# A chunked scan with scalar decays: the order of TensorE's work fixed by hand, one run of scan products per chunk

## The chip, the core and the metric

The kernel runs on one core of a Trainium2 chip as one program. The metric is the device time of one execution in microseconds. Before the change it is 3205.98 us, the median of three runs (3205.3 to 3206.26). The core's engines are named as the profile names them: PE (TensorE, with PEld for its weight loads), DVE (VectorE), ACT (ScalarE), POOL (GpSimd) and SP, whose queue issues most DMAs.

## The reference, cut to what matters

The program is three transformer-like blocks in sequence over 1024 positions and 1024 channels. The change touches the third block's second branch (`ssd_branch`): a causal depthwise convolution of width 4 with SiLU, a scan of 16 heads in 4 groups whose decays are scalars per head and position, and a gated group norm.

```python
xBC = silu(causal_depthwise_conv_3(xBC, conv_w, conv_b))   # xs (16 heads x 64), B and C (4 groups x 128)
dt = softplus(dt_raw + dt_bias);  A = -exp(A_log)
scores = einsum('bclhn,bcshn->bhcls', Ch, Bh) * exp(segsum(a))      # inside one chunk
y_diag = einsum('bhcls,bcshp->bclhp', scores, xd)
states = einsum('bclhn,bhcl,bclhp->bchpn', Bh, decay_states, xd)    # what a chunk adds to the state
y_off  = einsum('bclhn,bchpn,bhcl->bclhp', Ch, prev_states, exp(a_cs))
y = y_diag + y_off + Dh * xs
g = y * silu(z);  out = g * rsqrt(mean_group(g * g) + EPS) * norm_w
```

Beside it stands the S5 branch, of which only the last steps lie in the same stretch of time: a GELU per 128 channels (`gelu`) and a gated projection by `w_glu` (`glu`).

## The kernel before, in words

A weight of 1024 x 128 comes by DMA (`wraw`), is split by ACT (L147, `whi`) and POOL (L148, `wlo`) into two parts, and a dense half is 24 matmuls of 128 x 512 on PE (L157): 8 blocks of the contraction times three products. A group of four heads needs 12 dense halves: `conv_in` four times two (x, x, B, C) and the gate twice two (`rest`). Each half of `conv_in` leaves PSUM by a DVE product (L1710), then ACT, three DVE taps (L1715), ACT's tanh and a DVE product (L1718). A half of the gate is copied by ACT (L1743), turned by four PE transposes (L1745), scaled by ACT and passed through tanh. `to_time` turns x and B of a group in six PSUM banks of four transposes (L1728); each bank is copied out by DVE or ACT in turn (L1734, L1732), and there are two such banks (`tp`).

`scan` goes over 8 chunks of 128 positions. On PE a chunk has: the decay matrix (L1780 and two products L1786, whose operands ACT makes in L1785), B times C (L1790), the chunk's products for four heads (L1797, eight instructions), the state's output (L1802, two instructions, not in chunk 0) and the new state (L1810, two instructions, not in chunk 7). ACT's exponential and DVE's product (L1791) stand between L1786 and L1797; DVE's sum (L1814) stands between L1810 and the next chunk's L1802. `leave` turns the normed result (L1839) and writes it out.

The order of each engine's work is chosen by a planner, which runs through the program with durations of its own and takes, of what is ready by them, the instruction of the highest priority: what stands earlier in the program, and what is marked `high_priority` as if it stood 3000 places earlier. `scan(g)` is marked so; `project(g + 1)` (eight halves of `conv_in`, then `rest`) stands behind it and fills PE between the scan's products one matmul at a time. Dense halves also take one entry of a list (`K.tick`), by which the eight `gelu` steps are spread. A helper, `K.queue`, ties each PE instruction handed to it to the one before, while `K.queued` is set; in this branch it is not set. The engine's queue then keeps the planned order at run time.

In PSUM there are three `mm` banks for dense halves, two `aux`, two `tp` and one `stat`. `xt` and `bt` have one buffer, `M`, `sg`, `xd`, `st` and the gates `szt` two.

Of the kernel before, what the change touches and what calls it, by code (L numbers as in the profile page):

```python
# [1620 lines left out]
class SSD:  # L1621


    def __init__(self, K, norm, store, pd, pc):
        self.K, self.norm, self.store, self.pd, self.pc = K, norm, store, pd, pc
        self.mixd, self.groups = {}, {}
# [70 lines left out]
    def conv_in(self, g, i):  # L1697
# [6 lines left out]
        def ev(_, hf, ps):  # L1704
# [5 lines left out]
            nc.vector.tensor_mul(cp[:, 4:4 + HALF], ps, self.norm.row[hf])  # L1710
# [9 lines left out]
        K.dense([K.I["w_in_3"][col]], self.norm.y, ev)  # L1720

    def to_time(self, src, dst, at):
        K, nc = self.K, self.K.nc
        for b in range(2):
            pt = K.tp_bank()
            for i in range(4):
                c = 4 * b + i
                nc.tensor.transpose(pt[:, i * 128:(i + 1) * 128], src[:, c * 128:(c + 1) * 128], K.ident)  # L1728
# [7 lines left out]
    def rest(self, g, pool):  # L1736

        K, nc, y = self.K, self.K.nc, self.norm.y
        sz = pool.tile([128, 8, 256], F32, tag="szt", name=K.n("szt"), bufs=2)

        def ev(i, hf, ps):
            z = pool.tile([128, HALF], F32, tag="zf", name=K.n("zf"), bufs=1)
            nc.scalar.copy(z, ps)  # L1743
            for k in range(4):
                nc.tensor.transpose(ps[:, k * 128:(k + 1) * 128], z[:, k * 128:(k + 1) * 128], K.ident)  # L1745
            o = sz[:, 4 * hf:4 * hf + 4, i * 128:(i + 1) * 128]
            for k in range(4):
                nc.scalar.activation(o[:, k, :], ps[:, k * 128:(k + 1) * 128], AF.Copy, scale=self.zc[:, 4 * hf + k:4 * hf + k + 1])
            t2 = self.pc.tile([128, HALF], F32, tag="th", name=K.n("th"), bufs=2).rearrange("p (a b) -> p a b", b=128)
            K.act(t2, o, AF.Tanh)  # L1750
            nc.vector.scalar_tensor_tensor(o, t2, 1.0, o, op0=ALU.add, op1=ALU.mult)
            K.tick()

        K.dense([K.I["w_z_3"][2 * g + i] for i in range(2)], y, ev)
# [6 lines left out]
        self.groups[g] = t, xt, bt, sz  # L1761

    def project(self, g, pool):
        for i in range(4):
            self.conv_in(g, i)
        self.rest(g, pool)

    def scan(self, g, pool):
        K, nc = self.K, self.K.nc
        t, xt, bt, sz = self.groups[g]  # L1770
        CT, BT = t[3], t[2]
        hs = slice(4 * g, 4 * g + 4)
        h64 = lambda x: x.unsqueeze(2).to_broadcast((128, 4, 64))
        v64 = lambda x: x.rearrange("p (a b) -> p a b", b=64)
        st = None
        ss = pool.tile([128, 8], F32, tag="ss", name=K.n("ss"), bufs=2)
        for c in range(8):
            cs = slice(c * 128, (c + 1) * 128)
            ps = K.aux_bank()
            nc.tensor.matmul(ps.rearrange("p (a b) -> p a b", b=128), K.identb,  # L1780
                             self.future.unsqueeze(1).to_broadcast((128, 4, 128)), start=True, stop=False)
            for n, a in enumerate(self.ap):
                sg = pool.tile([128, 4, 128], F32R, tag="sg", name=K.n("sg"), bufs=2)
                for i in range(4):
                    nc.scalar.activation(sg[:, i, :], self.tri, AF.Copy, scale=a[:, c, 4 * g + i:4 * g + i + 1].bitcast(F32))  # L1785
                nc.tensor.matmul(ps, self.after1, sg.rearrange("p a b -> p (a b)"), start=False, stop=n == 1)  # L1786
            M = pool.tile([128, 4, 128], F32, tag="M", name=K.n("M"), bufs=2)
            K.act(M, ps.rearrange("p (a b) -> p a b", b=128), AF.Exp)
            pc = K.pp.tile([128, HALF], F32, tag="stat", name=K.n("cm"), bufs=1)
            nc.tensor.matmul(pc[:, 0:128], BT[:, cs], CT[:, cs], start=True, stop=True)  # L1790
            nc.vector.tensor_tensor(M, M, pc[:, 0:128].unsqueeze(1).to_broadcast((128, 4, 128)), op=ALU.mult)  # L1791
            x = xt[:, c, :]
            xd = pool.tile([128, 256], F32, tag="xd", name=K.n("xd"), bufs=2)
            nc.vector.tensor_tensor(v64(xd), v64(x), h64(self.dt[:, c, hs]), op=ALU.mult)
            yp = K.tp_bank()
            for i in range(4):
                nc.tensor.matmul(yp[:, i * 64:(i + 1) * 64], M[:, i, :], xd[:, i * 64:(i + 1) * 64], start=True, stop=True)  # L1797
            yo = pool.tile([128, 256], F32, tag="yo", name=K.n("yo"), bufs=2)
            nc.gpsimd.tensor_tensor(v64(yo), v64(x), h64(self.Dh[:, hs]), op=ALU.mult)
            nc.vector.tensor_add(yo, yp[:, 0:256], yo)  # L1800
            if c:
                nc.tensor.matmul(yp[:, 256:512], CT[:, cs], st, start=True, stop=True)  # L1802
                w = pool.tile([128, 256], F32, tag="yw", name=K.n("yw"), bufs=2)
                nc.vector.tensor_tensor(v64(w), v64(yp[:, 256:512]), h64(self.ecs[:, c, hs]), op=ALU.mult)
                nc.vector.tensor_add(yo, yo, w)
            if c < 7:
                xw = pool.tile([128, 256], F32, tag="xw", name=K.n("xw"), bufs=2)
                nc.gpsimd.tensor_tensor(v64(xw), v64(x), h64(self.dec[:, c, hs]), op=ALU.mult)
                pn = K.aux_bank()
                nc.tensor.matmul(pn[:, 0:256], bt[:, c, :], xw, start=True, stop=True)  # L1810
                s2 = pool.tile([128, 256], F32, tag="st", name=K.n("st"), bufs=2)
                if c:
                    nc.gpsimd.tensor_tensor(v64(s2), v64(st), h64(self.tot[:, c, hs]), op=ALU.mult)
                    nc.vector.tensor_add(s2, s2, pn[:, 0:256])  # L1814
                else:
                    nc.vector.tensor_copy(s2, pn[:, 0:256])
                st = s2
            z = sz[:, c, :]
            nc.gpsimd.tensor_mul(z, z, yo)
            nc.scalar.activation(yo, z, AF.Square, accum_out=ss[:, c:c + 1])  # L1820
        v = pool.tile([128, 8], F32, tag="ssv", name=K.n("ssv"), bufs=2)
        nc.vector.tensor_scalar(v, ss, 1.0 / 256, 1e-6, op0=ALU.mult, op1=ALU.add)
# [3 lines left out]
        if g < 2:  # L1826
            self.leaves(g, pool)

    def leaves(self, g, pool):
        for b in range(2):  # L1830
            for i in range(2):
                self.leave(g, b, i, pool)

    def turned(self, g, b, i):
# [3 lines left out]
        for k in range(4):  # L1838
            K.nc.tensor.transpose(pt[:, k * 128:(k + 1) * 128], sz[:, 4 * b + k, i * 128:(i + 1) * 128], K.ident)  # L1839
# [17 lines left out]
def block3(K, h, norm, s5, out):  # L1857
# [8 lines left out]
    with K.pool("sd") as pd, K.pool("sc") as pc:  # L1866
# [14 lines left out]
        with K.pool("s5") as ps5:  # L1881
# [47 lines left out]
            with K.pool("s5o") as po:  # L1929
                for bt in range(4):  # L1930
                    s5.outputs(X, U, po, bt)
                for i in range(4):
                    s5.outputs(X, U, po, 4 + i)
                    ssd.conv_in(0, i)
        with K.pool("ssd") as p:
            ssd.rest(0, p)
# [17 lines left out]
            K.rate = 1  # L1954
            for g in range(4):
                with K.tc.high_priority(offset=3000):
                    ssd.scan(g, p)
# [261 lines left out]
```

## Time and profile before

| | before |
|---|---|
| median of three runs | 3205.98 us |
| the profiled execution's own time | 3203.06 us |
| its span | 3201.3 us |
| mean granted PE clock | 0.977 |
| busy share of the span: PE, PEld, DVE, ACT, POOL | 95%, 76%, 60%, 40%, 43% |
| the four scans and what fills them | about 2462 to 2862 us of the span |

The span is the time from the first to the last instruction of the profiled execution. Busy shares are means over all three blocks; the stretch that the change touches is an eighth of the span. PE's rows overlap: a matmul's duration holds its way through the array, so what it costs in a stream is the distance from its start to the next one's. A wait in brackets is the idle time of that engine just before, and what ended it.

### The profile page before, as it was taken

What the parts mean: (1) busy time and instruction counts of PE and PEld (TensorE: products, weight loads), DVE (VectorE), ACT (ScalarE), POOL (GpSimd) and SP (SyncE); (2) the same over time, 40 slices, a digit from 0 to 9 for tenths busy, and PEclk for the clock granted to TensorE, in tenths of its full rate; (3) what the DMA queues carried; (4) which work ended last, traced back from release to release, by engine and by line L of the source; (5) the groups of instructions that cost most, each with busy time, mean ns of one, the idle gap of its engine ahead of it and who ended that gap; (6) DMA issues with size and microseconds to landing.
All of it is one profiled execution on the core that took longest, in us unless ns stands there. A gap on an engine that the chain in (4) does not pass through costs nothing. (4 is left out here: it accounts for less than half of the span.)

```text
span 3201.3 us, 41262 instructions
## 1 busy us (share of the span) xinstructions
PE 3045.4 (95%) x15370; PEld 2435.8 (76%) x15401; DVE 1921.3 (60%) x2902; ACT 1273.0 (40%) x2474; POOL 1382.7 (43%) x1069
## 2 busy tenths in 40 slices
PE   9999999899989999999997999999989989989997
PEld 7877677678777888777776777788778778778886
DVE  8994785453675364232165555684986887653434
ACT  3025565563252111111134656631114655643343
POOL 2323342114635444777743222442213553474455
PEclk9999999999989999999998999999999999989998
DMA  4132222134321112222221111346254221475322
GB/s 131 47 115 73 70 81 82 44 132 135 119 63 50 57 54 67 71 76 71 64 78 40 40 44 47 120 148 184 91 148 130 99 99 63 132 239 179 112 92 99
DMA packets 159737, 302.88 MB, mean 95 GB/s; under 512 B 23840, under 2 KB 66864, under 8 KB 159536
## 3 DMA queue, kind: packets, MB, share of 16 engines
q1 hardware_dynamic: 149104, 293.91, 28.4%
q10 hardware_dynamic: 10368, 6.30, 0.9%
q8 instruction: 122, 2.00, 0.3%
q14 instruction: 79, 0.65, 0.1%
q0 software_dynamic: 64, 0.03, 0.0%
HBM read 236.07 MB, written 64.09 MB: 94 GB/s over the span
## 5 line engine op out<-in xcount | busy, mean ns | idle before, releaser
L148 POOL TENSOR_TENSOR wlo<-wraw,whi 128x1024 fp32r<-128x1024 f32 (+1 forms) x309 | 752.0, 2435 | 1083.4 <-ACT whi L147 1065.3
L147 ACT CAST whi<-wraw 128x1024 fp32r<-128x1024 f32 (+1 forms) x313 | 309.1, 988 | 794.3 <-PE mm L157 581.5
L585 DVE SCALAR_TENSOR_TENSOR co<-cpad,conv_w,co 128x1024 f32<-128x1024 f32 x120 | 179.7, 1538 | 0.9
L780 DVE SCALAR_TENSOR_TENSOR e<-z,e 128x128 f32<-128x128 f32 (+7 forms) x64 | 52.6, 841 | 89.8 <-ACT e L219 89.0
L157 PE MATMUL mm<-mixh,whi 128*128 128x512 f32 x256 | 99.6, 393 | 3.0 <-DVE h L941 1.7
L157 PE MATMUL mm<-mixh,wlo 128*128 128x512 f32 x256 | 100.2, 393 | 1.2 <-POOL wlo L148 1.2
L1715 DVE SCALAR_TENSOR_TENSOR h<-cp,conv_w,h 128x512 f32<-128x512 f32 x96 | 89.6, 933 | 18.4 <-ACT h L1713 17.3
L157 PE MATMUL mm<-mixl,whi 128*128 128x512 f32 x256 | 99.9, 391 | 0.0
L781 DVE TENSOR_TENSOR_SCAN e<-e 128x128 f32<-128x128 f32 (+7 forms) x64 | 91.8, 1452 | 0.5
L219 ACT ACTIVATE e<-e 128x256 f32<-128x256 f32 (+7 forms) x128 | 83.1, 714 | 0.0
L337 DVE TENSOR_TENSOR sq<-sq,sq 128x512 f32<-128x512 f32 (+1 forms) x46 | 59.4, 1292 | 33.1 <-ACT sq L336 32.8
L941 DVE TENSOR_TENSOR h<-h,mm 128x512 f32<-128x512 f32 x64 | 43.4, 680 | 59.3 <-PE mm L157 59.3
L2033 DVE TENSOR_TENSOR h<-h,mm 128x512 f32<-128x512 f32 x32 | 22.0, 686 | 80.6 <-PE mm L157 80.6
L846 DVE TENSOR_TENSOR sz<-mm,row 128x512 f32<-128x512 f32 x32 | 22.0, 689 | 74.9 <-PE mm L157 74.9
L219 ACT ACTIVATE wt<-tp 128x512 f32<-128x512 f32 (+3 forms) x96 | 45.1, 500 | 51.8 <-PE tp L788 46.8
L1066 POOL TENSOR_TENSOR sw<-sw,rope_s 128x512 f32<-128x512 f32 x18 | 31.3, 1738 | 79.6 <-DVE sw L1065 79.6
L336 ACT ACTIVATE sq<-h 128x512 f32<-128x512 f32 x60 | 37.7, 629 | 68.5 <-POOL h L2065 29.8
L782 DVE TENSOR_TENSOR z<-z,e 128x128 f32<-128x128 f32 (+7 forms) x64 | 63.5, 1009 | 1.0
L157 PE MATMUL mm<-y01h,whi 128*128 128x512 f32 x146 | 60.7, 417 | 3.4 <-ACT y01h L68 2.5
L157 PE MATMUL mm<-y00h,whi 128*128 128x512 f32 x146 | 60.7, 416 | 3.3 <-DVE zt L1872 3.3
L774 ACT ACTIVATE e<-aux 128x384 f32<-128x384 f32 (+3 forms) x96 | 48.4, 505 | 33.6 <-PE aux L771 20.7
L219 ACT ACTIVATE p<-aux,m 128x256 f32<-128x256 f32 x84 | 39.0, 471 | 55.7 <-DVE m L1114 55.7
(1431 smaller groups left out, 10060.3 us busy)
## 6 DMA issues: line engine op xcount, KB each, us to landing
wraw<-w_in SPq DMA_DIRECT2D x76, 512.0 KB, 3.6
wraw<-w_in_even SPq DMA_DIRECT2D x53, 512.0 KB, 3.5
wraw<-w_out_even SPq DMA_DIRECT2D x40, 256.0 KB, 2.6
wraw<-w_in_odd SPq DMA_DIRECT2D x18, 512.0 KB, 3.5
sp_g<-gt SPq DMA_DIRECT2D x32, 256.0 KB, 2.0
g<-sp_g SPq DMA_DIRECT2D x32, 256.0 KB, 3.2
wraw<-w_out SPq DMA_DIRECT2D x16, 512.0 KB, 3.5
wraw<-w_out_odd SPq DMA_DIRECT2D x16, 512.0 KB, 3.5
```

Source lines behind the costliest of these rows:

```text
L147: self.nc.scalar.copy(hi, src)
L148: (eng or self.nc.gpsimd).tensor_sub(lo, src, hi.bitcast(F32))
L157: ins = self.queue(self.nc.tensor.matmul(ps, a[:, k, :], b[:, cols], start=first and n == 0, stop=last and n == total - 1)).ins
L219: ins = self.nc.scalar.activation(out, in_, func, **kw).ins
L337: (nc.vector if self.count > 5 else self.engines[i]).tensor_add(self.accs[i], self.accs[i], sq)
L585: nc.vector.scalar_tensor_tensor(o, cpad[:, tap:tap + S], cw[:, j, tap:tap + 1], o, op0=ALU.mult, op1=ALU.add)
L774: nc.scalar.activation(e[:, c0:c0 + n], bank[:, :n], AF.Abs)
L780: nc.vector.scalar_tensor_tensor(e[:, :L], z[:, :L], 0.0, e[:, :L], op0=ALU.max, op1=ALU.add)
L781: nc.vector.tensor_tensor_scan(e[:, rev], e[:, rev], e[:, rev], 0.0, op0=ALU.add, op1=ALU.bypass)
L782: nc.vector.tensor_sub(z[:, :L], z[:, :L], e[:, :L])
L941: nc.vector.tensor_add(h[e][:, half(hf)], h[e][:, half(hf)], ps)
L1715: nc.vector.scalar_tensor_tensor(oh, c(d), cw[:, ch, 3 - d:4 - d], oh, op0=ALU.mult, op1=ALU.add)
```

## The change: what it does, and the diff

The functions are cut anew. `decayed(g, c)` holds a chunk's decay matrix, B times C and M; `chunk(g, c)` holds the rest of a chunk, with the state's output placed directly behind the chunk's products; `normed(g)` holds the norm. `conv_in` and `gates` return lists of halves instead of computing them. The transposes of a gate half are put off (`turning`) until after the next run or the half after next. `scan(g)` now lays out the whole group: in each chunk one run (`chunk(c)`, `decayed(c + 1)`, put-off gate transposes), from chunk 2 on a `leave` of the group before, then one or two dense halves of group g + 1; at the end `normed`, the next group's first `decayed`, the last half and `to_times(g + 1)`. All PE instructions of the branch go through `K.queue` with `K.queued` set from the first `decayed` until scan 3 is laid out, so their order on PE is that of the program. DVE's product that empties a half of `conv_in` is ordered behind the last M product. The numbers of instructions on the engines and of DMAs stay as they were.

```diff
-            nc.vector.tensor_mul(cp[:, 4:4 + HALF], ps, self.norm.row[hf])
+            mul = nc.vector.tensor_mul(cp[:, 4:4 + HALF], ps, self.norm.row[hf])
+            if self.last is not None:
+                K.after(mul.ins, self.last)
...
-        K.dense([K.I["w_in_3"][col]], self.norm.y, ev)
+        return self.halfway(K.I["w_in_3"][col], lambda hf, ps: ev(None, hf, ps))
+
+    def halfway(self, src, ev):
+        K, w = self.K, []
+        def run(hf):
+            if hf == 0:
+                w.append(K.weight(src, 8, 128))
+            K.one(w[0], self.norm.y, hf, ev)
+        return [lambda: run(0), lambda: run(1)]
...
+    def gates(self, g, pool):
...
+            nc.scalar.copy(z, ps)
+            def turn():
+                for k in range(4):
+                    K.queue(nc.tensor.transpose(ps[:, k * 128:(k + 1) * 128], z[:, k * 128:(k + 1) * 128], K.ident))
...
+                K.tick()
+            self.turning.append(turn)
...
+    def turn_gates(self):
+        while self.turning:
+            self.turning.pop(0)()
...
+    def first_group(self, pool):
+        for step in self.gates(0, pool):
+            step()
+            self.turn_gates()
+        self.to_times(0, pool)
...
+        for i in range(4):
+            K.queue(nc.tensor.matmul(yp[:, i * 64:(i + 1) * 64], M[:, i, :], xd[:, i * 64:(i + 1) * 64], start=True, stop=True))
+        if c:
+            K.queue(nc.tensor.matmul(yp[:, 256:512], t[3][:, cs], st, start=True, stop=True))
...
+    def scan(self, g, pool):
+        K = self.K
+        fill = [[] for _ in range(8)]
+        if g < 3:
+            steps = [r for i in (0, 1, 2, 3) for r in self.conv_in(g + 1, i)] + [None] * 4
+            fill = [steps[0:2], steps[2:3], steps[3:5], steps[5:6], steps[6:8], steps[8:9], steps[9:11], steps[11:12]]
+        outs = [(b, i) for b in range(2) for i in range(2)] if g else []
+        zs = []
+        for c in range(8):
+            with K.tc.high_priority(offset=3000):
+                self.chunk(g, c, pool)
+                if c < 7:
+                    self.decayed(g, c + 1, pool)
+                self.turn_gates()
+            if outs and c > 1:
+                self.leave(g - 1, *outs.pop(0), pool)
+            if c == 5 and g < 3:
+                zs = self.gates(g + 1, pool)
+            if c == 7:
+                with K.tc.high_priority(offset=3000):
+                    self.normed(g, pool)
+                    if g < 3:
+                        self.decayed(g + 1, 0, pool)
+            for step in fill[c]:
+                if step is None:
+                    zs.pop(0)()
+                    if len(self.turning) > 1:
+                        self.turning.pop(0)()
+                else:
+                    step()
+            if c == 7 and g < 3:
+                with K.tc.high_priority(offset=3000):
+                    self.to_times(g + 1, pool)
...
             K.rate = 1
+            K.queued = True
+            with K.tc.high_priority(offset=3000):
+                ssd.decayed(0, 0, p)
             for g in range(4):
-                with K.tc.high_priority(offset=3000):
-                    ssd.scan(g, p)
-                if g < 3:
-                    if g:
-                        for e in range(4 * g - 4, 4 * g):
-                            K.bg += [(lambda: None)] * 2 + [lambda e=e: gelu(e)]
-                    ssd.project(g + 1, p)
+                if 0 < g < 3:
+                    for e in range(4 * g - 4, 4 * g):
+                        K.bg += [(lambda: None)] * 2 + [lambda e=e: gelu(e)]
+                ssd.scan(g, p)
                 if g == 2:
                     K.drain()
-                    ssd.leaves(2, p)
+            K.queued, K.tail = False, None
             mb = glu(K, ssd, p, pc, h, ygd, zsd, mad)
```

## Rows read from the trace of the kernel before

**Rows 1.** Windows, all engines: stretch, length, busy (instructions), PE clock, DMA share, GB/s.

```profile
2462.00:2785.00 323.00, 303.23 (x1493) 245.34 (x1491) 256.78 (x383) 197.14 (x474) 156.38 (x159) 0.99 0.28 93
2785.00:2819.00 34.00, 25.24 (x120) 20.43 (x121) 13.67 (x23) 18.96 (x53) 23.17 (x23) 0.76 0.63 208
2819.00:2862.00 43.00, 42.96 (x202) 35.24 (x202) 28.87 (x36) 18.72 (x41) 32.20 (x26) 0.99 0.71 234
2862.00:3195.00 333.00, 321.54 (x1442) 265.54 (x1440) 145.54 (x214) 131.71 (x178) 175.31 (x86) 0.98 0.38 124
```

**Rows 2.** Windows of the dense matmuls (L157) alone: PE, PEld, clock.

```profile
2462.00:2785.00 323.00, 241.92 (x931) 171.70 (x931) 0.99 0.28 93
2785.00:2819.00 34.00, 8.97 (x31) 5.66 (x32) 0.76 0.63 208
```

**Rows 3.** Waits of PE, 2462 to 2820: us in total, times, longest.

```profile
PE aux L1810 <- POOL wlo L148: 6.3, 1, 6.3
PE tp L1802 <- DVE yo L1800: 5.4, 6, 1.7
PE aux L1810 <- DVE st L1814: 4.3, 2, 2.3
```

**Rows 4.** Timeline of PE in scan 0: start, duration, instruction.

```profile
2490.54 0.59 PE L1802 MATMUL tp<-st,h 128*128 128x256 f32 x2
2490.97 0.38 PE L1780 MATMUL aux<-future,identb 128*128 128x512 bf16 x1
2490.99 0.58 PE L1786 MATMUL aux<-sg,after 128*128 128x512 f32 x1
2491.41 0.39 PE L157 MATMUL mm<-y30l,whi 128*128 128x512 f32 x1
2491.64 1.01 PE L1797 MATMUL tp<-xd,M 128*128 128x64 f32 x8
2492.46 0.48 PE L1786 MATMUL aux<-sg,after 128*128 128x512 f32 x1
2492.78 0.38 PE L1790 MATMUL cm<-h,h 128*128 128x128 f32 x2
2492.91 0.48 PE L157 MATMUL mm<-y30h,wlo 128*128 128x512 f32 x1
2493.23 0.39 PE L157 MATMUL mm<-y40h,whi 128*128 128x512 f32 x1
...
2497.33 0.39 PE L157 MATMUL mm<-y21h,whi 128*128 128x512 f32 x1
```

**Rows 5.** Timeline of PE: a bank of four transposes and the next matmul.

```profile
2759.22 0.60 PE L1728 MATMUL tp<-ident,h 128*128 128x128 f32 x4
2759.57 0.48 PE L157 MATMUL mm<-y40h,wlo 128*128 128x512 f32 x1
```

**Rows 6.** Timeline of PE in scan 1, behind a wait.

```profile
2628.32 1.22 PE L1810 MATMUL aux<-xw,bt 128*128 128x256 f32 x2 [2.34 <-DVE st L1814]
...
2629.76 0.63 PE L157 MATMUL mm<-y10h,whi 128*128 128x512 f32 x1
```

**Rows 7.** Timelines of PE and ACT: a turned bank and its copy.

```profile
2780.30 0.66 PE L1728 MATMUL tp<-ident,h 128*128 128x128 f32 x4 [1.48 <-ACT xt L1732]
...
2781.10 0.59 ACT L1732 COPY xt<-tp 128x512 f32<-128x512 f32 x1
```

**Rows 8.** Windows, all engines: scan 0.

```profile
2462.00:2545.00 83.00, 74.83 (x365) 59.57 (x364) 72.42 (x97) 52.16 (x129) 51.02 (x53) 1.00 0.25 83
```

**Rows 9.** Timeline of POOL ahead of the wait of 6.3 us.

```profile
2802.83 1.26 POOL L1993 TENSOR_TENSOR ya<-ya,yb 128x512 f32<-128x512 f32 x1 [6.86 <-DMA yb<-sp_zs]
```

**Rows 10.** Timelines of DVE and POOL at the end of scan 2.

```profile
2774.34 0.16 DVE L242 TENSOR_TENSOR rsq<-rsq,ssv 128x8 f32<-128x8 f32 x1
2776.27 2.41 DVE L242 TENSOR_TENSOR rsq<-rsq,ssv 128x8 f32<-128x8 f32 x1
...
2776.26 2.40 POOL L148 TENSOR_TENSOR wlo<-wraw,whi 128x1024 fp32r<-128x1024 f32 x1 [4.75 <-ACT whi L147]
```

More of the change, by code (lines that the diff above doesn't have):

```diff
@@ L1625, in __init__ @@
         self.K, self.norm, self.store, self.pd, self.pc = K, norm, store, pd, pc
-        self.mixd, self.groups = {}, {}
+        self.mixd, self.groups, self.state, self.last = {}, {}, {}, None
     def constants(self):
@@ L1734, in to_time @@
                 nc.vector.tensor_copy(o, i)
-    def rest(self, g, pool):
-        K, nc, y = self.K, self.K.nc, self.norm.y
+    def gates(self, g, pool):
+        K, nc = self.K, self.K.nc
         sz = pool.tile([128, 8, 256], F32, tag="szt", name=K.n("szt"), bufs=2)
+        self.groups[g] = [None, None, None, sz]
         def ev(i, hf, ps):
@@ L1760, in rest, with decayed @@
             self.to_time(t[i], xt, i * 128)
[L1761 to L1768, printed above, removed]
+        self.groups[g][0:3] = t, xt, bt
+    def first_group(self, pool):
[3 more added lines that the diff above has]
+        self.to_times(0, pool)
+    def decayed(self, g, c, pool):
+        K, nc = self.K, self.K.nc
+        t = [self.store[g % 2 * 4 + i] for i in range(4)]
+        cs = slice(c * 128, (c + 1) * 128)
+        ps = K.aux_bank()
+        K.queue(nc.tensor.matmul(ps.rearrange("p (a b) -> p a b", b=128), K.identb,
+                                 self.future.unsqueeze(1).to_broadcast((128, 4, 128)), start=True, stop=False))
+        for n, a in enumerate(self.ap):
+            sg = pool.tile([128, 4, 128], F32R, tag="sg", name=K.n("sg"), bufs=2)
+            for i in range(4):
+                nc.scalar.activation(sg[:, i, :], self.tri, AF.Copy, scale=a[:, c, 4 * g + i:4 * g + i + 1].bitcast(F32))
+            K.queue(nc.tensor.matmul(ps, self.after1, sg.rearrange("p a b -> p (a b)"), start=False, stop=n == 1))
+        pc = K.pp.tile([128, HALF], F32, tag="stat", name=K.n("cm"), bufs=1)
+        K.queue(nc.tensor.matmul(pc[:, 0:128], t[2][:, cs], t[3][:, cs], start=True, stop=True))
+        M = self.state[g, c] = pool.tile([128, 4, 128], F32, tag="M", name=K.n("M"), bufs=2)
+        K.act(M, ps.rearrange("p (a b) -> p a b", b=128), AF.Exp)
+        self.last = nc.vector.tensor_tensor(M, M, pc[:, 0:128].unsqueeze(1).to_broadcast((128, 4, 128)), op=ALU.mult).ins
@@ L1769, in scan, with chunk @@
+    def chunk(self, g, c, pool):
         K, nc = self.K, self.K.nc
         t, xt, bt, sz = self.groups[g]
-        CT, BT = t[3], t[2]
-        hs = slice(4 * g, 4 * g + 4)
+        hs, cs = slice(4 * g, 4 * g + 4), slice(c * 128, (c + 1) * 128)
         h64 = lambda x: x.unsqueeze(2).to_broadcast((128, 4, 64))
         v64 = lambda x: x.rearrange("p (a b) -> p a b", b=64)
[L1775 to L1800, printed above, removed]
-            if c:
[L1802 to L1820, printed above, removed]
@@ new lines, in chunk @@
+        if c == 0:
+            self.ss = pool.tile([128, 8], F32, tag="ss", name=K.n("ss"), bufs=2)
+            self.st = None
+        M, st = self.state.pop((g, c)), self.st
+        x = xt[:, c, :]
+        xd = pool.tile([128, 256], F32, tag="xd", name=K.n("xd"), bufs=2)
+        nc.vector.tensor_tensor(v64(xd), v64(x), h64(self.dt[:, c, hs]), op=ALU.mult)
+        yp = K.tp_bank()
+        for i in range(4):
+            K.queue(nc.tensor.matmul(yp[:, i * 64:(i + 1) * 64], M[:, i, :], xd[:, i * 64:(i + 1) * 64], start=True, stop=True))
@@ L1933, in block3 @@
                     s5.outputs(X, U, po, 4 + i)
[L1934 removed]
+                    for step in ssd.conv_in(0, i):
+                        step()
         with K.pool("ssd") as p:
[L1936 removed]
+            ssd.first_group(p)
             Dc = K.const("s5_D_3", (128, 8), pool=pd)
```

55 lines of the change are left out of this document (36 added, 19 removed).

## The prediction

> **What bounds the kernel now.** I read the windows first, to see in which stretch TensorE does not work, then its waits, then its timeline there. Behind 2819 us PE is busy in 42.96 of 43 us and then in 321.5 of 333, with the end of the program in the last of it [rows 1]: whatever reaches that point earlier ends earlier, so the question is only when the work done by 2819 is done. Ahead of it PE is idle for 19.8 us of 323 and for 8.8 of 34, the latter at a mean clock of 0.76 [rows 1]. The waits name the scan's own small products, each held up by VectorE or GpSimd: 6.3 us for one new state behind a weight's split, 5.4 in six waits of the state's output, 4.3 in two of new states [rows 3]. In the scans VectorE is nearly as full as PE: 72.4 against 74.8 of 83 us [rows 8].
>
> How much of the stretch is work? I count from the first matmul of group 1's convolution, at 2462.0, to the start of glu's fifth half, at 2819.4: 357.4 us. In it lie 962 dense matmuls by the windows [rows 2], which is 36 halves of groups 1 to 3 and 4 halves of glu, 960 in all. From 2493.23 to 2497.33 eighteen of them follow each other, 0.228 apart [rows 4], so they cost 218.9. A full run of one chunk, from start to start [rows 4]: eight L1797 0.82, L1802 0.43, L1810 of the same shape 0.43 (taken as equal), L1780 0.02, two L1786 0.42 + 0.32, L1790 0.13, together 2.57. Scans 0 to 2 and five chunks of scan 3 are 29 runs, less four L1802 of first chunks and three L1810 of last ones: 74.5 - 3.0 = 71.5. A turned bank is 0.35 [rows 5], and 44 banks (by the code 18 of to_time and two left of group 0, 12 of gates, 12 of leave) are 15.4. Sum 305.8. So 51.6 us are lost now: 28.6 idle, and 23.0 in returns and at the lower clock. A return is the first dense matmul behind a small product, 0.32 in place of 0.228 [rows 4], and nothing keeps the planner from putting each product of a chunk between other matmuls. As to the clock: behind a wait of 2.34 us a dense matmul's row is 0.63 long against 0.39 [rows 6, 4], the lower of the two levels, 1.2 in place of 2.4 GHz.
>
> **The change part by part.** The instructions are the same, so the 305.8 of PE stay; the sum is what is lost beside them.
>
> *One run per chunk.* Per group about 11 returns are left (8 runs, three put-off gate turns), and a dozen in scan 3, some 45 at 0.09: 4.0 us.
>
> *State output behind the products, new state behind that.* Between the run that makes a state and the one that uses it there is now at least one half, 24 x 0.228 = 5.5 us, for one sum on VectorE; the same 5.5 us lie between L1786 and the next L1797 for the exponential and M's product. The waits of rows 3 go, if these engines get to it in time. What is late next is VectorE: the stretch to 2785 has 256.8 us of it [rows 1], and nearly all of it must now fit in some 300. It is not spread evenly. The eight convolution halves, each with five VectorE passes, stand in chunks 0 to 4, the four light gate halves in 5 to 7. Where VectorE lags by more than those 5.5 us, M is late, and behind L1797 waits all of PE, since no dense matmul may pass; before, the fill could pass where the planner had put it. The added order (emptying a half behind M's product) queues the taps, and so the next halves' banks, behind the same M. No row shows this order. From below it is 0 (three `mm` banks and 5.5 us hide it), from above three groups at the idle time of scan 0, 83 - 74.83 = 8.2 each [rows 8], 25. I take 10, nearer to 0 than to 25, since GELU's share lies in groups 0 and 1 only and the waits of rows 3 partly came from the order.
>
> *Turning a group, to_times.* Before, the six banks lie between dense matmuls. Now they stand in one piece behind the last gate half, with nothing to fill. With two banks the copies set the pace: 0.80 us from a bank's first transpose to its copy and 0.59 for the copy [rows 7], say 1.5 per pair, 4.5 for three pairs, then one more VectorE product (taken as long as a copy, 0.7) before the next L1797. Of these 5.2 us 2.1 are work [rows 5], so 3.1 are idle at least. VectorE has the norm of the old group in the same place, so I take 4.0, at most 6. There are four such places, the first at the start of scan 0, where the first convolution half filled before: 16 us (12.4 to 24), and 2 more there, as the first half also begins later. The clock may fall behind each [rows 6]: 3 in all (0 to 6).
>
> *Gate turns put off.* They no longer wait for ACT's copy; that wait is small now and stays at nothing, and if ACT were late, the run in front covers it.
>
> *Scan 3.* No halves are laid between its runs; glu's matmuls are not tied and fill where the planner puts them, as before. The fourth `leave` of group 2 now comes in chunk 5, and glu's spare buffers (the old gates) come free only then, so what empties glu's halves waits for that; two th buffers and three banks allow five halves, 27 us, until then, about as long as five chunks take. Before, the place lost 20 us: POOL waited 6.86 for a DMA [rows 9], the next weight's split stood behind it, and five chunks' products were done at idle 8.8 and the lower clock [rows 1]. The same queue of POOL can stall again, but with two chunks left. Between 0 and 20 I take 9. SP's queue carries the same DMAs; those of `leave` move behind gy loads and ahead of glu's a and b, and they have the length of a chunk to land.
>
> Sum of losses: 4 + 10 + 16 + 2 + 3 + 9 = 44, against 51.6: 7.6 us gained. The profiled execution took 3203.06 (its span is 3201.3), so it would take 3195.5; the median of the runs is 2.9 above the profiled one, which gives 3198.4, and I say **3198**.
>
> **The rivals.**
>
> *Slower: VectorE's M becomes the gate of all PE work.* For it: scan 0 with VectorE at 87% [rows 8], and its convolution passes now packed in five chunks. Price: 25 in place of 10, at the lower clock more often (5 in place of 3), scan 3 at 12: 64, that is 12.4 lost, 3218. It decides from where PE's waits on VectorE in runs exceed the 10 taken by 7.6, or 2.5 a group. Against it: none of PE's waits on VectorE is longer than 2.3 us [rows 3]. A VectorE instruction of 128x8, 0.16 long, took 2.41 when a split of a weight began on GpSimd 0.01 us before it and ran 2.40 [rows 10]; 18 splits in three groups at 2.25 each would be 40 us, on top of what the other engine hides. The Trainium skill (SBUF — State Buffer, Who interferes with whom) says why: an instruction of VectorE with two SBUF inputs is shut out until a GpSimd instruction that reads SBUF ends. By that rule alone, with every split striking an M or a state sum, the kernel would be slower still, at 3206 + 40 - 8 = 3238; by the row it is one strike in many, and of this rival's chance 0.05 goes to it.
>
> *Much faster: the turnings are at their lower bound, VectorE keeps up and scan 3 runs full.* 4 + 12.4 + 3 + 5 = 24, 27.6 gained, 3178. For it: each wait of rows 3 comes from order, not from load.
>
> *Nothing gained: order fixed on PE alone.* ACT, VectorE, GpSimd and SP keep the planner's order, made with its own durations; the waits move from the small products to the banks and weights, and the turnings eat the rest: 51.6, 3206. For it: POOL's 6.86 is such an error of order.
>
> **How the numbers follow.** Forecast 0.40, own range 3191 to 3206; slower 0.25; much faster 0.15; nothing gained 0.20. All bounds together give losses of 16 to 81, or 3171 to 3235; the range that leaves 2 in 10 out is 3174 to 3222. What a measurement of this kernel can tell from no change is about 0.2%, 6.4 us. Faster by more: 0.8 of 0.40, 0.15 and 0.15 of 0.20, together 0.50. Within: 0.2 of 0.40 and 0.7 of 0.20, 0.22. Slower: 0.25 and 0.15 of 0.20, 0.28.
>
> **What would show it.** After: L1802 and L1810 with hardly a wait, each L1797 followed by L1802; returns seen as rows of 0.48 in tens, not hundreds; waits of L1728 on DVE and ACT copies of about 4 us in each of four places, with L157 rows of 0.63 behind them if the clock falls; waits of L1797 on L1791 for the first rival; POOL's L1993 waiting on a DMA only late in scan 3. The prediction is wrong if the stretch from group 1's first half to glu's fifth is longer than 357, or shorter than 340.

## The result and the profile after: 1% slower, lost in places where TensorE has nothing it may do

After the change the kernel takes 3237.9 us (median of four runs, 3233.34 to 3238.44) against 3206.12 before on the same chip: a ratio of 1.0094, 95% interval 1.0078 to 1.0111. I forecast 3198, faster, with a range that ended at 3222. The sign and the range were both wrong. The profiled execution took 3238.44 (span 3235.2, mean granted clock 0.970), against 3203.06 before (span 3201.3).

The windows that answer to [rows 1], all engines of the changed kernel (stretch, length, busy, clock, DMA share, GB/s):

```profile
2462.00:2785.00 323.00, 294.01 (x1431) 244.59 (x1430) 236.18 (x361) 187.91 (x457) 156.35 (x157) 0.95 0.25 82
2785.00:2857.00 72.00, 56.73 (x262) 46.50 (x260) 35.34 (x70) 37.19 (x96) 36.88 (x37) 0.82 0.48 162
2857.00:3229.00 372.00, 358.10 (x1592) 294.59 (x1592) 163.11 (x228) 144.67 (x197) 198.87 (x100) 0.98 0.42 139
```

The loss is ahead of 2857: PE's idle time to 2785 rises from 19.8 to 29 us, its clock falls from 0.99 to 0.95, and the weak place behind 2785 is twice as long, at a clock hardly better. The waits of PE in the stretch, which answer to [rows 3] (us in total, times, longest):

```profile
PE tp L1832 <- DVE M L1814: 20.0, 8, 3.4
PE tp L1832 <- DVE xd L1829: 8.4, 3, 4.3
PE tp L1741 <- DVE bt L1747: 5.8, 2, 5.5
PE mm L157 <- ACT th L219: 3.5, 1, 3.5
PE tp L1741 <- DVE xt L1747: 2.0, 1, 2.0
```

(L1832 is the chunk's products, L1797 before; L1741 the turning's transposes, L1728 before.) The waits of [rows 3] on the state are gone, as forecast. In their place stand M, and at the turnings xd and bt.

The same 40 dense halves as in the prediction's stretch lie here from 2474.60 to 2857.36. (By the halves' operands the ends are group 1's second half and glu's sixth, in both kernels, one later than I called them; the count of 40 stands.) First row: all engines; second: L157 alone.

```profile
2474.60:2857.36 382.76, 341.06 (x1637) 283.03 (x1636) 262.81 (x419) 217.26 (x532) 184.47 (x184) 0.93 0.29 97
2474.60:2857.36 382.76, 227.93 (x961) 179.10 (x960) 0.93 0.29 97
```

The work in it, by the prediction's prices: 218.9 for 960 matmuls, 75.8 for 31 runs without what first and last chunks lack, 14.7 for 42 banks, 309.4. So 73.4 us are lost, 41.7 of them idle, against 51.6 before; some 5 more are lost at the first turning ahead of it: from group 0's first gate half to that end 39.0 us go by (2435.6 to 2474.6) against 31.9 before, and 2.1 of the difference is chunk 0's run. Together these two stretches account for 33 of the 33.9 us by which the spans differ; what lies ahead of them is 5.0 us longer, what lies behind them 4.1 shorter.

Three losses can be seen in rows. **The turnings.** Between the last gate half and the next products, windows of the three places and of scan 3, and then L157 alone in the third place:

```profile
2564.57:2575.42 10.85, 4.91 (x26) 3.93 (x24) 9.99 (x20) 4.20 (x7) 5.03 (x4) 0.69 0.03 6
2674.21:2684.32 10.11, 3.44 (x26) 2.52 (x24) 9.36 (x22) 3.16 (x5) 4.86 (x5) 0.83 0.34 105
2779.08:2796.44 17.36, 13.74 (x73) 11.41 (x72) 14.29 (x33) 8.86 (x16) 5.29 (x3) 1.00 0.51 167
2796.44:2857.36 60.92, 48.91 (x219) 40.11 (x220) 26.81 (x51) 32.19 (x89) 34.15 (x37) 0.78 0.46 155
...
2779.08:2796.44 17.36, 12.10 (x49) 8.79 (x48) 1.00 0.51 167
```

Each holds 2.1 us of transposes and the third two dense halves (10.9): 8.8, 8.0 and 4.4 lost, 21.1 in all. VectorE is busy in 9.99 of the first 10.85 us. Its timeline there, between two rows of PE's and with one of POOL's (start, duration, instruction, idle before and what ended it), then three rows of VectorE and one of PE in the second place:

```profile
2564.57 1.03 PE L1741 MATMUL tp<-ident,h 128*128 128x128 f32 x8
...
2564.30 0.75 DVE L2014 SCALAR_TENSOR_TENSOR ya<-yb,s_D,ya 128x512 f32<-128x512 f32 x1 [4.52 <-DMA yb<-s5uD]
2564.97 0.68 DVE L1814 TENSOR_TENSOR M<-M,cm 128x512 f32<-128x512 f32 x1
2565.57 0.69 DVE L1767 SCALAR_TENSOR_TENSOR szt<-th,szt 128x512 f32<-128x512 f32 x1
2566.17 0.59 DVE L1861 TENSOR_SCALAR ssv<-ss 128x8 f32<-128x8 f32 x1
...
2568.14 2.27 DVE L241 SCALAR_TENSOR_TENSOR rsq<-rsq 128x8 f32<-128x8 f32 x1
2570.34 0.68 DVE L1747 COPY bt<-tp 128x512 f32<-128x512 f32 x1
...
2568.05 2.34 POOL L148 TENSOR_TENSOR wlo<-wraw,whi 128x1024 fp32r<-128x1024 f32 x1
...
2571.07 3.87 PE L1741 MATMUL tp<-ident,h 128*128 128x128 f32 x16 [5.46 <-DVE bt L1747]
...
2675.46 2.22 DVE L242 TENSOR_TENSOR rsq<-rsq,ssv 128x8 f32<-128x8 f32 x1
...
2680.24 3.60 DVE L1864 TENSOR_SCALAR szt<-szt,rsq 128x256 f32<-128x256 f32 x8
2683.76 0.74 DVE L1829 TENSOR_TENSOR xd<-xt,dt 128x256 f32<-128x256 f32 x2
...
2684.32 1.94 PE L1832 MATMUL tp<-xd,M 128*128 128x64 f32 x8 [4.29 <-DVE xd L1829]
```

The copy that PE waits for is the eighth row of VectorE's from 2564.30 on (two small steps of the norm are left out above), behind GELU's first product, which had waited for its load, M, a gate's product and the old group's norm. One small step of the norm is drawn out beside a split on GpSimd: 2.27 us, where the same instruction took 0.17 at 2571.32. The other two places have such a step too, of 2.22 (above) and 2.36 us. In the second place PE waits for xd, which stands behind the eight products of the norm (3.60). The length of these places does not hang on GELU: without it (run 12) they take 10.1, 10.1 and 17.6 us. The four banks behind the first wait take 3.87 us in place of 1.40: the lower level of the clock.

**M in scans 0 and 1** (11.8 of the 20.0 us). M's chain at one of the four waits, a row each of PE, DVE and ACT:

```profile
2513.52 1.83 PE L1832 MATMUL tp<-xd,M 128*128 128x64 f32 x8 [3.43 <-DVE M L1814]
...
2503.06 0.75 DVE L2014 SCALAR_TENSOR_TENSOR ya<-yb,s_D,ya 128x512 f32<-128x512 f32 x1 [2.50 <-DMA yb<-s5uD]
2508.13 1.49 DVE L2019 SCALAR_TENSOR_TENSOR yc<-yb,ya 128x512 f32<-128x512 f32 x1 [0.15 <-ACT yb L219]
2512.79 0.68 DVE L1814 TENSOR_TENSOR M<-M,cm 128x512 f32<-128x512 f32 x1
...
2509.88 0.57 ACT L219 ACTIVATE M<-aux 128x512 f32<-128x512 f32 x1
```

ACT's exponential starts 5.5 us after PE's last product for it ended (2504.4), since ACT's queue too stands behind steps of GELU there; VectorE's product comes 2.3 us after the exponential. The eight products take 1.83 behind this wait, 1.00 elsewhere. All four waits are of chunks 4 and 6, behind a chunk with one dense half. From the wait to the next dense half the mean granted clock is 0.51 to 0.64 behind the three waits of 3.07 to 3.43 us, and 1.00 behind the fourth, of 1.86. Windows of a two-half and a one-half chunk, in scan 1 with GELU and in scan 2 without:

```profile
2597.70:2611.90 14.20, 14.16 (x70) 11.92 (x71) 11.13 (x17) 9.43 (x22) 10.84 (x12) 1.00 0.17 57
2611.90:2624.10 12.20, 8.77 (x47) 7.13 (x45) 10.55 (x16) 5.88 (x15) 4.80 (x6) 0.95 0.44 150
...
2709.40:2723.50 14.10, 14.10 (x71) 11.83 (x70) 11.09 (x16) 7.01 (x16) 5.93 (x7) 1.00 0.17 54
2723.50:2732.10 8.60, 8.60 (x47) 7.30 (x46) 6.79 (x13) 5.95 (x16) 3.74 (x6) 1.00 0.17 66
```

PE needs 8.6 us for the one-half chunk; VectorE's 10.55 do not fit into it (1.5 of them are one product of GELU drawn out beside a split, 2.63 where the shortest of its form took 1.09). It is a matter of where the work falls: over the two chunks together VectorE has 21.7 us for the 22.7 that PE takes in scan 2, but in the first chunk it is idle for 3.1.

**Scan 3.** Its window above holds 72 dense matmuls (16.4), eight runs without what the ends lack (18.8) and five banks (1.8: four leaves and the last put-off gate turn), 37.0 in 60.9 us: 23.9 lost. Two parts of it, ahead of glu's third half and behind its fifth, hold nearly all of the loss, 7.7 and 15.0 us. Their windows, then the end on PE, then ACT and the DMA queue:

```profile
2796.44:2809.24 12.80, 10.35 (x36) 8.29 (x37) 8.80 (x15) 8.78 (x24) 9.21 (x11) 0.52 0.53 186
2832.67:2857.36 24.69, 15.13 (x70) 12.14 (x69) 11.22 (x23) 10.65 (x31) 13.68 (x15) 0.75 0.67 221
...
2832.67 1.00 PE L1832 MATMUL tp<-xd,M 128*128 128x64 f32 x8
2833.51 0.65 PE L1834 MATMUL tp<-st,h 128*128 128x256 f32 x2
2833.99 0.59 PE L1846 MATMUL aux<-xw,bt 128*128 128x256 f32 x2
...
2837.96 1.97 PE L1832 MATMUL tp<-xd,M 128*128 128x64 f32 x8 [2.03 <-DVE M L1814]
...
2851.24 1.65 PE L1832 MATMUL tp<-xd,M 128*128 128x64 f32 x8 [2.69 <-DVE M L1814]
...
2857.36 0.80 PE L157 MATMUL mm<-y00h,whi 128*128 128x512 f32 x1 [3.51 <-ACT th L219]
...
2856.62 0.69 ACT L219 ACTIVATE th<-mm,s_b_glu 128x512 f32<-128x512 f32 x1 [3.68 <-DMA sp_ma<-th]
...
2844.33 0.32 SPq L2058 DMA_DIRECT2D spare<-sp_yg  x1
...
2850.78 0.38 SPq L2063 DMA_DIRECT2D sp_ma<-th  x1
```

In the first part, which follows a wait of 3.62 us for xd, PE has two runs and a gate turn, 5.1 us of work, waits 2.17 for M, and works at the lower level. After glu's fifth half no dense matmul starts until 2857.36: th waits for its store (2850.78), that for a product of `spare`, and its load (2844.33) for the fourth `leave`. The first three rows of PE answer to [rows 4]: the state's output follows the products and the new state follows it, with no wait.

### The profile page after: what moved, and what is told of

It is laid out like the page before. It is cut to its first block, busy times and chain, and to the rows that moved or that the text cites. A ratio compares the mean times of both kernels' runs of the same rounds, so it can differ in the third digit from the quotient of the medians.

```text
span 3235.2 us, 41296 instructions
## 1 busy us (share of the span) xinstructions
PE 3061.2 (95%) x15401; PEld 2452.8 (76%) x15401; DVE 1907.9 (59%) x2902; ACT 1273.7 (39%) x2474; POOL 1371.0 (42%) x1069
## 4 chain that ended last, share of the span: by engine, by line
PE 55%; DVE 24%; ACT 6%; issue 6%; DMA 5%; POOL 3%; SPq 0%; ACTq 0%; DVEq 0%; POOLq 0%
PE mm L157 46%; DVE co L585 5%; ACT p L219 2%; POOL wlo L148 1%; ACT p L1122 1%; DVE m L1111 1%; DVE e L781 1%; PE aux L768 1%; PE mm L797 1%; DVE rec L1582 1%; PE tp L788 1%; DMA yb<-s5uD 1%; ACT whi L147 1%; PE mm L599 1%; DVE h L1717 1%
## 5 line engine op out<-in xcount | busy, mean ns | idle before, releaser
L148 POOL TENSOR_TENSOR wlo<-wraw,whi 128x1024 fp32r<-128x1024 f32 (+1 forms) x309 | 737.0, 2387 | 1122.6 <-ACT whi L147 1088.1
L157 PE MATMUL mm<-mixh,whi 128*128 128x512 f32 x256 | 100.3, 396 | 1.7 <-DVE h L941 1.5
L157 PE MATMUL mm<-mixh,wlo 128*128 128x512 f32 x256 | 100.6, 394 | 0.3 <-POOL wlo L148 0.3
L157 PE MATMUL mm<-mixl,whi 128*128 128x512 f32 x256 | 100.3, 392 | 0.0
L157 PE MATMUL mm<-y00h,whi 128*128 128x512 f32 x146 | 63.1, 432 | 8.4 <-ACT th L219 3.5
L1832 PE MATMUL tp<-xd,M 128*128 128x64 f32 x256 | 38.6, 301 | 31.1 <-DVE M L1814 20.0
L1832 PEld LDWEIGHTS tp<-xd,M 128*128 128x128 f32 x256 | 37.1, 217 | 36.9 <-DVE M L1814 23.6
L157 PE MATMUL mm<-y01h,whi 128*128 128x512 f32 x146 | 61.1, 420 | 3.0 <-ACT y01h L68 2.6
```

Of the source, the lines that this page charges most:

```text
L148: (eng or self.nc.gpsimd).tensor_sub(lo, src, hi.bitcast(F32))
L157: ins = self.queue(self.nc.tensor.matmul(ps, a[:, k, :], b[:, cols], start=first and n == 0, stop=last and n == total - 1)).ins
L1832: K.queue(nc.tensor.matmul(yp[:, i * 64:(i + 1) * 64], M[:, i, :], xd[:, i * 64:(i + 1) * 64], start=True, stop=True))
```

## Experiments

Ratios are to the kernel before, run on the same chip, with 95% intervals; the changed kernel is at 1.0094, and 0.001 is 3.2 us. The runs are from five chips, and the changed kernel itself was not run again beside them, so a gain against 1.0094 is known to some 6 to 9 us. Theory A: the tie of all PE instructions turns each late operand into idle time of PE. Rivals: VectorE has too much work in any order (B); the turnings alone (C); what exactly makes M late (D); scan 3 (E).

**1. No tie.**
```diff
-            K.queued = True
```


> Only the tie between TensorE's instructions is taken off in the scan branch; chunks, runs, put-off gate transposes and the pin of the emptying product stay. Theory A (the fixed order itself costs: a late M or a late copy in a turning holds up all dense matmuls): the planner lets dense matmuls pass again, idle time in the scans falls to about 30 us, time 3200 to 3212. Rival B (VectorE's load and the new layout, pieces and pin cost, not the tie): stays at 3228 or more.

Measured 0.9968 (0.9956 to 0.9981). Theory A holds, and more than it asked: without the tie the rest of the change is faster than before. VectorE's instructions are the same and its waits for GELU's loads are longer (21.4 us from 2462 to 2800, 14.8 with the tie); but PE waits less, as its waits on M show, here from 2400 to 2950 (20.0 in eight with the tie):

```profile
PE tp L1832 <- DVE M L1814: 10.1, 4, 6.5
```

**2. M two chunks ahead** (the main lines).
```diff
-                if c < 7:
-                    self.decayed(g, c + 1, pool)
+                if c < 6:
+                    self.decayed(g, c + 2, pool)
+                elif g < 3:
+                    self.decayed(g + 1, c - 6, pool)
...
```


> M is made two chunks ahead in place of one (three M buffers), the order stays fixed. Theory A: the eight waits of the chunk's products on M (20.0 us) go, and some of the half clock behind them, so 20 to 27 us less than the changed kernel: 3211 to 3218. Rival B (VectorE simply has too much to do): the waits move to xd, the copies or the state's sums, gain under 8: 3230 or more. Rival C (the turnings of a group are the main loss): the turnings keep their 11, 10 and 17 us, gain near 20 at most.

1.0058 (1.0037 to 1.0079): 11.5 us, known to 9. No wait of L1832 on M is left, so 20.0 us of waits gave some 11.5. The rest came back elsewhere, from 2400 to 2950: waits for the normed gates (10.1 in two, of which the changed kernel has none), for the state (5.3, none before), for xd (13.7 in four, 11.0 before) and for a gate's copy (4.2, 1.5 before).

**3. The turning taken apart.**
```diff
...
+            if c == 7 and g < 3:
+                with K.tc.high_priority(offset=3000):
+                    turns.pop(0)()
+                K.hooks = [turns.pop(0), lambda: None]
+            for n, step in enumerate(fill[c]):
+                if c == 6 and g < 3 and n:
+                    turns = self.to_times(g + 1, pool)
+                    with K.tc.high_priority(offset=3000):
+                        turns.pop(0)()
...
```


> The turning of a group is taken apart: B's two banks between the two halves behind chunk 6, two of x's behind chunk 7 ahead of the last gate half, two inside that half. Rival C (the three turnings, 11, 10 and 17 us from the last gate half to the next chunk's products with 2.1 us of work each, are the main loss): some 4 us are left of each, 20 to 28 us gained, 3210 to 3218. Theory A (M late is the main loss): the first products of the next scan then wait for M or xd instead, since VectorE and ScalarE are late with everything there; gain under 10, 3228 or more.

1.0028 (1.0015 to 1.0041): 21 us, as much as the rows give for the three places. M's waits grew to 25.5 in ten, so C is the larger part, not the whole.

**4. GELU's loads a dense half earlier.** The loads of a piece are issued at the tick before its arithmetic, one piece a tick.

> GELU's two loads per piece are issued one dense half ahead of their use, same buffers, same places of the rest. Theory A in its finer form (VectorE stands at GELU's first instruction, waiting for its DMA, and M's product is queued behind it): VectorE's 14.8 us of waiting on these DMAs in the scans fall under 4, half or more of the 20.0 us of waits on M go, 10 to 20 us gained, 3218 to 3228. Rival B (load): within 4 us of 3238, the waits on M stay.

1.0086 (1.0064 to 1.0108), within the noise of no gain. VectorE's waits on these loads fell to 5.9 us, and PE's waits on M rose to 26.1. My finer form falls: the load at the head of VectorE's queue was not what made M late.

**5. GELU held to its own groups and to chunks with two halves; 6. the same with the turning taken apart.**
```diff
-                    nc.vector.scalar_tensor_tensor(a, b, Dc[:, e:e + 1], a, op0=ALU.mult, op1=ALU.add)
+                    K.after(nc.vector.scalar_tensor_tensor(a, b, Dc[:, e:e + 1], a, op0=ALU.mult, op1=ALU.add).ins, ssd.last)
...
-                        K.bg += [(lambda: None)] * 2 + [lambda e=e: gelu(e)]
+                        K.bg += [(lambda: None)] * (1 if e % 4 == 0 else 3 if e % 4 == 3 else 2) + [lambda e=e: gelu(e)]
```


> The changed kernel with GELU held to its own groups and to chunks 0, 2, 4 and 6: its first product per piece is ordered on VectorE behind the last M product laid out, so that no piece is pulled ahead into scan 0, and it falls behind the runs with two dense halves. Theory D (M is late because GELU's VectorE work, pulled ahead by the planner, falls in the chunks with one dense half, where VectorE has no slack): waits of the chunk's products on M fall from 20.0 to under 7 us, 12 to 20 us gained, ratio to before 1.003 to 1.006. Rival B (any GELU beside the convolution makes M late, wherever it stands): waits on M stay above 15 and only move from scan 0 to scan 2, ratio 1.008 or more. A cost that could hide the gain: glu's first half waits for the last GELU.

1.0107 (1.0089 to 1.0125): no gain. Waits on M are 21.8 us in ten: none in scan 0, now without GELU, 5.7 us in scan 1, 5.4 in scan 2, which now has it, and 10.7 in scan 3. They moved with the work, as the rival said; the one-half chunk still gets what the two-half chunk leaves over.

> The turning taken apart as in the run of that edit alone (ratio 1.0028) and GELU held as in the run beside this one. If the two losses add, both gains come: ratio 0.997 to 1.000. If VectorE's lateness only changes its place, ratio 1.002 or more.

1.0050 (1.0031 to 1.0070), no better than the turning alone.

**7. Without the order of the emptying product behind M.**
```diff
-            if self.last is not None:
-                K.after(mul.ins, self.last)
```


> The changed kernel without the order of the emptying product behind the last M product. If that order is what lets M be late less often, M's waits grow and the ratio is above 1.011; if it makes the convolution's banks and taps late, and so the next M, the ratio is under 1.007; I expect neither: within 0.2% of the changed kernel, 1.008 to 1.011.

1.0100 (1.0085 to 1.0115), as expected: no cost and no gain of this order can be told.

**8. No tie and the turning taken apart.**

> No tie on TensorE (ratio 0.9968 by itself) and the turning taken apart. Where the turnings cost only because nothing may pass, this adds nothing: within 0.15% of 0.9968. If the copies of xt and bt are late for another reason, their earlier place gains 3 to 8 us more: 0.994 to 0.996.

0.9981 (0.9971 to 0.9990): nothing added. By these runs a turning costs only where nothing may pass it.

**9. Group 2's leaves in chunks 0 and 1 of scan 3; 10. the same without a tie.**
```diff
-            if outs and c > 1:
-                self.leave(g - 1, *outs.pop(0), pool)
+            for _ in range(2 if g == 3 else c > 1):
+                if outs:
+                    self.leave(g - 1, *outs.pop(0), pool)
```


> The changed kernel with group 2's four leaves laid into chunks 0 and 1 of scan 3 in place of chunks 2 to 5. Theory E (in scan 3 the glu halves stop because their spare buffers, the old gates, come free only with the fourth leave at 2843 us; TensorE then does the last three runs at the lower clock and waits 3.5 us for th): the glu halves go on, scan 3 loses 8 to 15 us less, ratio 1.005 to 1.007. Rival (the glu halves wait for the gy loads and weights anyway, or the leaves hold up the first runs): 1.0085 or more.

1.0067 (1.0049 to 1.0084): 8.7 us, known to 8, near the lower edge of theory E.

> The same move of the leaves with no tie on TensorE (0.9968 by itself, where th is waited for as well, ACT's 10.1 us in scan 3). If theory E holds there too, 4 to 10 us more: 0.9935 to 0.9955. If the planner fills the place with other work anyway: 0.996 to 0.998.

0.9971 (0.9958 to 0.9984): nothing. glu's ninth half starts at 2837.8 in place of 2849.9, but PE then waits for a weight whose split stands in GpSimd's queue behind one of glu's products, which had waited for its load (a row of PE, two of POOL):

```profile
2853.33 0.80 PE L157 MATMUL mm<-y01h,wlo 128*128 128x512 f32 x1 [4.00 <-POOL wlo L148]
...
2846.25 4.28 POOL L2061 TENSOR_TENSOR spare<-spare 128x512 f32<-128x512 f32 x1 [4.27 <-DMA spare<-sp_yg]
2850.50 5.11 POOL L148 TENSOR_TENSOR wlo<-wraw,whi 128x1024 fp32r<-128x1024 f32 x2
```

**11. All three mends, order fixed (2, 3 and 9).**

> The order stays fixed; the turning is taken apart, M is made two chunks ahead and the leaves of group 2 come early. If the three losses are separate and add up, 21 (turnings) + 20 (M) + 8 to 15 (scan 3) less: ratio 0.995 to 0.999. If VectorE's load beside GELU is what counts, M's part only changes its place as in the run of that edit alone (11 us gained): ratio 0.999 to 1.003.

1.0008 (0.9998 to 1.0018): 27.6 us, in the range of the second case. The three alone sum to 41 (11.5 + 21 + 8.7), but that sum is known only to some 15, so that the parts overlap is likely and not shown.

**12. GELU left out** (its arithmetic and loads; a copy in DRAM stands for it, so this kernel does not compute the reference).

> The changed kernel without GELU's arithmetic and loads (a copy in DRAM stands in its place). Theory D' (VectorE's GELU work on top of the convolution's, wherever it stands, makes M late): waits of the products on M in scans 0 and 1 fall from 11.8 us (the four of these two scans) to under 2, those of scan 3 stay (8.2), each pair of chunks with convolution takes about 21.8 us as in scan 2, and 15 to 25 us are gained: ratio 1.002 to 1.005. Rival (the planner's order on VectorE or ScalarE makes M late without GELU too): waits on M in scans 0 and 1 stay above 6, ratio 1.006 or more. The turnings keep most of their length.

1.0034 (1.0017 to 1.0050). No wait on M is left in scans 0 to 2; the pair of chunks that took 26.4 us takes 22.7, like scan 2's:

```profile
2587.00:2601.10 14.10, 14.10 (x71) 11.85 (x70) 11.09 (x16) 7.02 (x16) 5.92 (x7) 1.00 0.11 34
2601.10:2609.70 8.60, 8.60 (x47) 7.30 (x46) 6.78 (x13) 5.96 (x16) 3.74 (x6) 1.00 0.18 68
```

So GELU's work on top of the convolution's is what makes M late there; GELU has work on ACT and GpSimd too, and this run does not part their share from VectorE's. The turnings keep their length.

**13. Only the small products tied, dense halves free.**
```diff
+            queued, K.queued = K.queued, False
             K.one(w[0], self.norm.y, hf, ev)
+            K.queued = queued
```


> The changed kernel with the dense halves of the scan branch taken out of the tie; the small products (scan, turnings, leaves) keep their fixed order among themselves. Theory A (what costs is that a dense matmul may not pass a waiting small product): ratio 0.996 to 0.9985, as with no tie at all. Rival (the order of the small products themselves costs, or gains): above 1.002 or under 0.995.

1.0038 (1.0016 to 1.0061): 18 of the 40 us between tie and no tie. Against the expectation, the fixed places of the small products cost too: in the profiled execution scan 3 runs as in the changed kernel (2792.7 to 2850.7), and M is waited for 23.0 us in 14. That execution took 3236.0 us, the longest of seven with a median of 3224.6, so its waits are rather too large for the ratio.

**14. The tie cut once per scan, behind chunk 0's run; 15. the same with mends 2 and 9.**
```diff
+            if c == 0:
+                K.tail = None
```


> The tie stays, but is cut once in each scan behind chunk 0's run, so that the next group's first two convolution halves may stand before or within the turning ahead of it. Theory C (the turnings lose some 30 us because nothing may fill them): 15 to 25 us gained, ratio 1.0015 to 1.0045. Rival (VectorE's and ScalarE's copies are late whatever fills, and chunk 0's or 1's products wait instead): 1.006 or more.

1.0051 (1.0034 to 1.0069): 14 us, a little less than expected. The two turnings that a convolution half can fill are filled; M's waits rise to 30.8, and the third turning has no such half.

> The cut, M two chunks ahead, and the early leaves of group 2. If each takes what it took by itself (3.6 for M, 2.7 for the leaves, the cut's own part, in thousandths): 0.996 to 0.999. If they overlap: 1.000 to 1.003.

0.9978 (0.9964 to 0.9991): as far as these intervals tell, the parts add up here (their sum would give 0.9988), and an order fixed but for one opening per group is faster than before.

**16. No tie with mends 2 and 9.**

> No tie, M two chunks ahead, early leaves. Without a tie the waits on M are 10.1 us, 6.5 of them one wait in scan 3's last chunk: M two ahead should take most, 3 to 8 us on 0.9968: 0.9945 to 0.996. If a wait on M costs nothing where dense matmuls pass: 0.9965 to 0.998.

0.9968 (0.9953 to 0.9983): nothing, though the products' waits on M fall to 0.7 us. Waits of B times C, whose one bank M's product empties, rise from 1.4 to 4.4, and waits on the state from 1.8 to 9.9.

**17. No tie, gates turned at once; 18. only the small products tied, with mends 2 and 9.**

> No tie, and each gate half is turned at once, as before the change, in place of behind the next run or half. If putting off the transposes is what makes the untied kernel faster than before (0.9968), this returns to 0.999 to 1.001. If the gain is from the new layout of halves and chunks (priorities), it stays at 0.9955 to 0.998; I expect the second, since TensorE's waits on the gate's copy (L1757) are 1.5 us in the changed kernel and as small before.

0.9986 (0.9976 to 0.9996), between the two ranges that I gave, against 0.9968 (0.9956 to 0.9981). The intervals overlap: putting off the gate transposes may be worth half of what the untied kernel gains over before; that is not settled, nor where the rest comes from. The order of the emptying product was not tried without the tie.

> Only the small products are tied; M is made two chunks ahead and group 2's leaves come early. If what is left of the loss (1.0038) is M and scan 3: 0.996 to 0.999. If it is the fixed order of the small products as such: 1.001 to 1.004.

0.9987 (0.9975 to 0.9999): 16 us on run 13. Its rest was mostly M made too late and the late leaves, which this run does not part, and not the order of the small products as such.

The lowest ratios are those of the untied variants, 1 and 16, at 0.9968, which 10 (0.9971) and 15 (0.9978) cannot be told from. To take only the tie away is the smallest edit that gets there.

## Why the prediction was wrong, step by step

| term of the lost time | taken | measured |
|---|---|---|
| returns | 4 | 2.8 (62 changes of kind on PE, half of them returns, at 0.09) |
| turnings, three later ones | 12 | 21.1 |
| gate turns put off | 0 | 1.5 (one wait on a gate's copy) |
| first turning and late first half | 6 | some 5 |
| M late, scans 0 and 1 | 10 | 11.8 idle |
| lower clock | 3 | some 12 in scans 0 to 2: what is left of 73.4 |
| scan 3 | 9 | 23.9 |
| sum | 44 | some 78 |

**Right**: the stretch is where the time is made; the waits of [rows 3] go; returns (226 changes of kind before, 62 now, some 7 us gained); M is next to be late. **The rival came in part**: PE's waits on M are 20.0 us, over the 17.6 from which I said it decides, but only 11.8 of them lie in the three groups that it was about, near the 10 taken; 8.2 lie in scan 3. I gave it 0.25 and priced it at 64 lost; 78 were, and what carried the loss there are the turnings, the clock and scan 3, which it too had at 16, 5 and 12. Its chance was too low for a reason in the rows. I set 256.8 us of VectorE against 300 and took 10 for the unevenness, but a tied order asks the question per chunk: 10.55 in 8.6.

**Mis-sized, the turnings.** 1.5 us for a pair of banks supposed that VectorE copies as soon as a bank is full, as in [rows 7]. I raised 3.1 idle to 4.0 for the norm in the same place, at most 6; 8.8, 8.0 and 4.4 were lost. In the first place the norm, M, a gate's product, GELU and the copies together fill 9.99 of 10.85, and in the second the norm's eight products alone (3.60) stand ahead of xd. Undone alone: 21 us.

**Mis-sized, the clock.** I took [rows 6] for single events, 3 us. Three of the four waits on M in scans 0 and 1, and the longest wait at each of the three turnings, are followed by work at the lower of the two levels, with a mean granted clock of 0.50 to 0.64: 1.83 for 1.00, 3.87 for 1.40.

**Mis-sized, scan 3.** I counted five halves, 27 us, until the fourth leave, and took that for about five chunks. Five halves were right, but two of them had been used up in the third turning, so three were left to fill eight chunks (23.9, over my bound of 20). Moving the leaves gave back 8.7; the 7.7 ahead of glu's third half I had not foreseen.

**The figure of 3238** that I worked out from the Trainium skill (SBUF — State Buffer, Who interferes with whom) came true by luck, for another reason. Against VectorE's shortest row of the same line and shape, 20 instructions are drawn out by more than 0.8 us in this stretch (by 31.0 us in all) and 25 were before (by 40.5): single strikes sit in the chains (one step of the norm in each turning, 2.2 to 2.4 us), but their number did not rise. Nor could they strike where I put them. The rule as I gave it is of instructions with two SBUF inputs; M's product and the state's sum each read one operand from a PSUM bank, and none of them is drawn out in either kernel: M's products take 0.67 to 0.69 us (28 before, 30 after), the state's sums 0.40 to 0.42.

**Missing altogether** was the test that run 1 makes: what is the fill worth that may pass? I said that no dense matmul may pass, and priced only the lateness of M by it. This is the step that failed: in the sum, each place without fill was priced as if the operand came soon and only M could be late. Without the tie dense matmuls stand in these places, and the kernel takes 40 us less, at the same work (1.0094 to 0.9968).

## What to carry to other kernels

Before an order is written out by hand for one engine, go through it chunk by chunk and compare what each feeding engine must do in that chunk with the chunk's length; means over the stage hide the chunk that doesn't fit. Wherever the fixed order leaves a place without fill (a turning, the end of a stage), price it with the queue of the engine that feeds it, everything that stands ahead included, and with the lower clock behind it. A tie that is cut once per group, with M made two chunks ahead and the leaves moved forward, kept the order otherwise and lost nothing (0.9978).

## What the runs showed that I had not expected

Waits removed gave back perhaps half of themselves (11.5 of 20.0 us, known to 9), since the lateness came back at the next place; in the untied kernel taking the products' waits on M from 10.1 to 0.7 us gave nothing. And shortening VectorE's waits on a DMA at the head of its queue (14.8 to 5.9 us) changed no time that the runs can tell.
